# Gate and up chunks with ScalarE and VectorE in the program's order, and other pairs with seven products

## The chip, the cores and the metric

One core of a Trainium2 chip runs the kernel. The metric is device microseconds (us) of one execution, the median over runs; lower is better. TensorE is called PE here, VectorE DVE, ScalarE ACT, GpSimd POOL and SyncE SP, as in the profile.

## The reference

Two layers of a residual trunk on 256 tokens of width 2048, all in float32. Each layer normalises, projects, runs two kinds of attention, projects back, and then runs a SwiGLU. Only the SwiGLU matters here:

```python
def swiglu(h, w_gate, w_up, w_down):
    return (jax.nn.silu(h @ w_gate) * (h @ w_up)) @ w_down
...
        h = rms_norm(x, pre_ffn_norm[l])
        f = swiglu(h, w_gate[l], w_up[l], w_down[l])
        x = x + rms_norm(f, post_ffn_norm[l])
```

`w_gate` and `w_up` are 2048 x 5632, `w_down` is 5632 x 2048.

## The kernel before

**Precision.** Every float32 operand is split into a rounded part `hi` (written by ACT, L181 and L205) and a rest `lo = x - hi` (written by DVE, L182 and L207). A product of two blocks is three matmuls, hi by hi, hi by lo and lo by hi (`product`, L730). So each weight that PE uses goes through one ACT and one DVE instruction of 128x1024 first.

**Tiling of gate and up.** The 5632 columns are 11 chunks of 512. A chunk contracts 8 *K pairs* (`kp` 0 to 7) of 2 x 128 rows. For one pair the tokens (2 tiles of 128), the two row blocks and the two matrices make a 2 x 2 by 2 x 2 block product. `eight` (L837) takes it as 8 products, 24 matmuls. `seven` (L847) takes it as 7 products, 21 matmuls, from sums of blocks. The pairs in `SEVEN` (L36; chunk 0: `FIRST_SEVEN`, L37) go through `seven`. For them the sums of the tokens come once per layer from `pair_sums` (L830), placed in chunk 0 by `FORM_AT`, and the sums of the weights come from `mixed_weights` (L172) each time. The order of its steps on the two engines is:

1. ACT `hi` of gate (L205), DVE `lo` of gate (L207); ACT `hi` of the tile T (L181), DVE `lo` of T (L182). T is up with one half of gate added by a second DMA from POOL (`summed`, L164).
2. DVE L186 makes the sum t2 in T; DVE L187 and L188 overwrite the gate tile with two more sums.
3. ACT `Th` of t2 and DVE `Tl` of t2 (128x512); ACT `Th` and DVE `Tl` of the gate tile (128x1024). The first `Th` reads what L186 wrote, the second what L188 wrote, and each `Tl` reads its `Th`.

**Banks.** An odd and an even chunk use four PSUM banks each. The other four hold the shared products p1, p6, p7, q5 of the seven-product pairs. After the last such pair `shared_part` (L767) joins them with one ACT copy (L770) and four DVE instructions (L771 to L774); those banks then take the next chunk's sums.

**End of a chunk (L876 to L893).** Per token tile: DVE adds gate's bank (L880), ACT takes SiLU (L881), DVE adds up's bank (L882) and multiplies (L883). `flip`, started `DEFER_ACT` ticks later, transposes the result on PE (L889), into a bank that the next chunk's shared products use as well, and ACT copies it out (L890).

**Weights.** `fetch` (L149) puts the loads on SP's queue, 512 KB each, in the order of use; T loads are put up to `EARLY` places ahead. `feed` (L195) puts the splits ahead of the matmuls by `LOOKAHEAD` = 4 tiles, two pairs. Buffers: 4 `raw`, 6 `hi`, 6 `lo`, 3 T, 2 `Th`, 2 `Tl`. A buffer is given to a new tile when the old one's last reader is done.

**Down (L901 to L986).** Two halves of two column chunks each, 22 K pairs; the pairs in `DOWN_SEVEN` (L40) go through `seven_products`, the others through `down`. The last three pairs of the second half are the tail.

**What sets the order.** Tile's scheduler orders each engine's instructions by its own estimate of when they can start, unless a block is under `tc.manual_schedule`, in which the named engines keep the order in which the program records the instructions. Before, only the end of the output projection (L806) is under it.

Of the kernel before, what the change touches and what calls it, by code (L numbers as in the profile page):

```python
# [24 lines left out]
FF = 5632  # L25
CW = 512
# [6 lines left out]
URGENT = 50  # L33
TAIL = 3
KP_O = (4, 5, 6, 7, 0, 1, 2, 3)
SEVEN = (2, 4, 5, 6)  # L36
FIRST_SEVEN = (4, 6)  # L37
FIRST_ORDER = (0, 1, 3, 2, 4, 5, 6, 7)
FORM_AT = {1: 4, 3: 6, 4: 5, 5: 2}
DOWN_SEVEN = (2, 5, 8, 11, 14, 17)  # L40

WARM = 13
LEVEL = 232
# [7 lines left out]
def weight_order():  # L51
# [3 lines left out]
    def queue_pair(name, l, kp, c):  # L55
        order.append((name, l, kp, c))
        return len(order) - 1
# [3 lines left out]
    for l in range(L):  # L61
# [15 lines left out]
        for c in range(FF // CW):  # L77
            for kp in FIRST_ORDER if c == 0 else range(KT // 2):
                lay["gate"][c, kp] = queue_pair("w_gate", l, kp, c)
                lay["up"][c, kp] = queue_pair("w_up", l, kp, c)  # L80
                if kp in (FIRST_SEVEN if c == 0 else SEVEN):
                    sevens.add(lay["up"][c, kp])
        for half in range(2):
            for kp in range(FF // P // 2):
                for c in (2 * half, 2 * half + 1):
                    lay["down"][c, kp] = queue_pair("w_down", l, kp, c)
                if kp in DOWN_SEVEN:
                    sevens.add(lay["down"][2 * half + 1, kp])
# [17 lines left out]
def kernel(  # L106
# [30 lines left out]
    def four_banks(odd, names):  # L137
        makers = (bank, bank, bank, last_bank) if odd else (acc_bank,) * 4
        return [make(n) for make, n in zip(makers, names)]
# [75 lines left out]
    def weights(i, ahead):  # L215
        feed(i + 1 + ahead)
        return ready[i]
# [19 lines left out]
    def new_x_pool(nm):  # L237
        if x_pool[0] is not None:
            x_pool[0].release()
        x_pool[0] = tc.alloc_tile_pool(name=nm, bufs=1, side="right", reuse_waits="tile")  # L240
        return x_pool[0]
# [112 lines left out]
    def start(gen, n=1):  # L354
        running.append([clock[0] + n, gen])
# [381 lines left out]
    def token_sums(pool, spool, bufs, a11, a12, a21, a22, nm):  # L737

        s = pool.tile([P, 4, P], F32, tag="t2", name=f"s{nm}")
        nc.vector.tensor_tensor(out=s[:, 0, :], in0=a21, in1=a22, op=ALU.subtract)  # L740
        nc.vector.tensor_tensor(out=s[:, 1, :], in0=s[:, 0, :], in1=a11, op=ALU.subtract)
        nc.vector.tensor_tensor(out=s[:, 2, :], in0=a11, in1=a21, op=ALU.subtract)
        nc.vector.tensor_tensor(out=s[:, 3, :], in0=s[:, 1, :], in1=a12, op=ALU.add)
        sh = spool.tile([P, 4, P], F32R, tag="sh", bufs=bufs, name=f"sh{nm}")
        nc.scalar.activation(sh, s, AF.Copy)
        sl = spool.tile([P, 4, P], F32R, tag="sl", bufs=bufs, name=f"sl{nm}")
        nc.vector.tensor_tensor(out=sl, in0=s, in1=sh.bitcast(F32), op=ALU.subtract)
        return [(sh[:, j, :], sl[:, j, :]) for j in range(4)]
# [18 lines left out]
    def shared_part(extra, w):  # L767

        p1, p6, p7, q5 = extra
        nc.scalar.copy(w[0], p1)  # L770
        nc.vector.tensor_tensor(out=w[1], in0=p6, in1=w[0], op=ALU.add)  # L771
        nc.vector.tensor_tensor(out=w[2], in0=p7, in1=w[1], op=ALU.add)
        nc.vector.tensor_tensor(out=w[1], in0=q5, in1=w[1], op=ALU.subtract)
        nc.vector.tensor_tensor(out=w[3], in0=q5, in1=w[2], op=ALU.subtract)  # L774

    xT = None
    for l in range(L):
# [52 lines left out]
        def pair_sums(kp):  # L830
            f = pool.tile([P, 2, S], F32, tag="t2", name=f"f{l}_{kp}")
            for kk in range(2):
                st = xT[2 * kp + kk]
                nc.vector.tensor_tensor(out=f[:, kk, :], in0=st[:, 0, :].bitcast(F32), in1=st[:, 1, :].bitcast(F32), op=ALU.add)
            forms[kp] = token_sums(pool, gu, len(SEVEN), f[:, 0, 0:P], f[:, 1, 0:P], f[:, 0, P:S], f[:, 1, P:S], f"{l}_{kp}")

        def eight(banks, c, kp, toks, first, last):  # L837
            g, u = weights(plan[l]["gate"][c, kp], LOOKAHEAD), weights(plan[l]["up"][c, kp], LOOKAHEAD)
            for kk in range(2):
                st = xT[2 * kp + kk]  # L840
                for t in toks:
                    tick()
                    stat = (st[:, 0, t * P : (t + 1) * P], st[:, 1, t * P : (t + 1) * P])
                    for col, (hi, lo) in enumerate((g, u)):
                        product(banks[2 * t + col], stat, (hi[:, kk, :], lo[:, kk, :]), first and kk == 0, last and kk == 1)

        def seven(banks, extra, c, kp, first, last):  # L847
            hi, lo = weights(plan[l]["gate"][c, kp], LOOKAHEAD)
            m = weights(plan[l]["up"][c, kp], LOOKAHEAD)
            e, o = xT[2 * kp], xT[2 * kp + 1]  # L850
            a11, a12, a22 = (e[:, 0, 0:P], e[:, 1, 0:P]), (o[:, 0, 0:P], o[:, 1, 0:P]), (o[:, 0, P:S], o[:, 1, P:S])
            seven_products(banks, extra, forms[kp], a11, a12, a22, hi, lo, m, first, last)

        for c in range(FF // CW):
            banks = four_banks(c % 2, [f"c{q}_{l}_{c}" for q in ("11", "12", "21", "22")])
            mine = FIRST_SEVEN if c == 0 else SEVEN
            order = FIRST_ORDER if c == 0 else tuple(range(KT // 2))
            if c == 0:
                for t in range(NT):
                    for kp in order[:2]:  # L860
                        eight(banks, c, kp, (t,), kp == order[0], False)
                order = order[2:]
            extra = None
            for n, kp in enumerate(order):
                if c == 0 and n in FORM_AT:
                    pair_sums(FORM_AT[n])
                if kp not in mine:
                    eight(banks, c, kp, range(NT), kp == 0, kp == order[-1])
                    continue
                if kp == mine[0]:  # L870
                    extra = four_banks(1 - c % 2, [f"{q}_{l}_{c}" for q in ("p1", "p6", "p7", "q5")])
                seven(banks, extra, c, kp, kp == mine[0], kp == mine[-1])
                if kp == mine[-1]:
                    w = [pool.tile([P, CW], F32, tag="t2", name=f"w{j}_{l}_{c}") for j in range(4)]
                    shared_part(extra, w)
            at = pool.tile([P, 4, S], F32, tag="act", bufs=FF // CW, name=f"act{l}_{c}")  # L876
            act.append(at)
            sg = [w[0], w[2]]
            for t, u in ((0, w[1]), (1, w[3])):
                nc.vector.tensor_tensor(out=sg[t], in0=banks[2 * t], in1=sg[t], op=ALU.add)  # L880
                nc.scalar.activation(sg[t], sg[t], AF.Silu, scale=rs[t][:, 0:1])  # L881
                nc.vector.tensor_tensor(out=u, in0=banks[2 * t + 1], in1=u, op=ALU.add)  # L882
                nc.vector.scalar_tensor_tensor(out=sg[t], in0=u, scalar=rs[t][:, 0:1], in1=sg[t], op0=ALU.mult, op1=ALU.mult)  # L883

            def flip(sg=sg, at=at, c=c):
                for t in range(NT):
                    pb = (bank if c % 2 else acc_bank)(f"actT_ps{l}_{c}_{t}")
                    for j in range(4):
                        nc.tensor.transpose(pb[:, j * P : (j + 1) * P], sg[t][:, j * P : (j + 1) * P], ident)  # L889
                    nc.scalar.copy(at[:, :, t * P : (t + 1) * P], pb.rearrange("p (k q) -> p k q", k=4))  # L890
                    yield 1

            start(flip(), DEFER_ACT)  # L893
        gu.release()
        mix_pool[:] = new_x_pool(f"sums{l}"), 2, plan[l]["down"][3, FF // P // 2 - 1] + 1
        dn = tc.alloc_tile_pool(name=f"dn{l}", bufs=4, reuse_waits="tile")
# [6 lines left out]
        for half in range(2):  # L903
            split, forms = {}, {}

            def prep(kp):
# [7 lines left out]
                split[kp] = (jh, jl)  # L914
                if kp in DOWN_SEVEN:
                    a11, a12, a21, a22 = src[:, 0, 0:P], src[:, 1, 0:P], src[:, 0, P:S], src[:, 1, P:S]
# [23 lines left out]
            def down_seven(kp):  # L940
# [5 lines left out]
                m = weights(plan[l]["down"][cc[1], kp], LOOKAHEAD)  # L946
                seven_products(got, extra, forms[kp], a11, a12, a22, hi, lo, m, kp == DOWN_SEVEN[0], kp == DOWN_SEVEN[-1])

            tail = TAIL if half == 1 else 0
            for kp in range(nkp - tail):  # L950
                if kp not in DOWN_SEVEN:
                    down(kp, range(NT))
                    continue
                if kp == DOWN_SEVEN[0]:
                    extra = four_banks(half, [f"{q}_d{l}_{half}" for q in ("p1", "p6", "p7", "q5")])
                down_seven(kp)
                if kp == DOWN_SEVEN[-1]:
                    for t in range(NT):
# [84 lines left out]
```

## Time and profile before

| | |
|---|---|
| median of 3 runs | 2235.16 us (2232.64 to 2235.85) |
| the profiled execution | 2239.96 us, span 2237.9 us |
| granted clock of PE in it | 0.997 |
| PE busy | 2200.9 us, 98% of the span |
| DVE busy | 1789.1 us, 80% |
| ACT busy | 1309.5 us, 59% |
| DMA | 452 MB, mean 202 GB/s |
| gate and up, layer 0 and 1 | about 400 to 885 us and 1515 to 2005 us |
| down, layer 0 and 1 | about 885 to 1125 us and 2005 to 2238 us |

A matmul of 128x512 is listed with some 0.39 us, but the next one starts 0.227 us after it: matmuls overlap. A share of 98% for PE therefore hides little idle time, and its mean over all stages says nothing on how close DVE is to its limit in one of them. The stages have to be read one by one.

### The profile page before, as it was taken

What the parts mean: (1) busy time and instruction counts of PE and PEld (TensorE: products, weight loads), DVE (VectorE), ACT (ScalarE), POOL (GpSimd) and SP (SyncE); (2) the same over time, 40 slices, a digit from 0 to 9 for tenths busy, and PEclk for the clock granted to TensorE, in tenths of its full rate; (3) what the DMA queues carried; (4) which work ended last, traced back from release to release, by engine and by line L of the source; (5) the groups of instructions that cost most, each with busy time, mean ns of one, the idle gap of its engine ahead of it and who ended that gap; (6) DMA issues with size and microseconds to landing.
All of it is one profiled execution on the core that took longest, in us unless ns stands there. A gap on an engine that the chain in (4) does not pass through costs nothing.

```text
span 2237.9 us, 28440 instructions
## 1 busy us (share of the span) xinstructions
PE 2200.9 (98%) x10057; PEld 1802.2 (81%) x10057; DVE 1789.1 (80%) x2531; ACT 1309.5 (59%) x1937; POOL 132.0 (6%) x184
## 2 busy tenths in 40 slices
PE   9999999999999999999999999999999999999998
PEld 7888888777887888788878888887777887878886
DVE  6666555899988999989776665558999999998897
ACT  6545554665655656656565455546665566566664
POOL 1100000000000000000010000000000000000000
PEclk9999999999999999999999999999999999999999
DMA  8555455576776676766555544556677677666673
GB/s 290 189 167 164 160 190 183 186 223 209 226 242 199 212 251 190 228 214 205 193 184 171 168 162 160 188 186 192 206 218 237 218 222 234 221 203 222 203 232 132
DMA packets 133326, 452.05 MB, mean 202 GB/s; under 512 B 15296, under 2 KB 15808, under 8 KB 132672
## 3 DMA queue, kind: packets, MB, share of 16 engines
q1 hardware_dynamic: 117488, 421.91, 55.2%
q0 software_dynamic: 15552, 28.32, 7.6%
q8 instruction: 79, 1.29, 0.2%
q14 instruction: 63, 0.52, 0.1%
q10 hardware_dynamic: 144, 0.02, 0.0%
HBM read 448.09 MB, written 2.10 MB: 201 GB/s over the span
## 4 chain that ended last, share of the span: by engine, by line
PE 71%; DVE 13%; DMA 6%; issue 4%; ACT 4%; POOL 0%; DVEq 0%; ACTq 0%; SPq 0%; POOLq 0%
PE in L380 7%; PE in L382 7%; PE in L381 7%; DMA raw<-in_weights_in_turn_dram 5%; PE c L733 5%; PE c L734 5%; PE c L735 5%; PE dn L938 5%; PE dn L936 5%; PE dn L935 4%; DVE lo L207 3%; DVE Tl L182 2%; PE o L382 2%; PE o L381 2%; PE o L380 2%
## 5 line engine op out<-in xcount | busy, mean ns | idle before, releaser
L207 DVE TENSOR_TENSOR lo<-raw,hi 128x1024 fp32r<-128x1024 f32 x675 | 824.1, 1225 | 311.4 <-ACT hi L205 307.3
L205 ACT ACTIVATE hi<-raw 128x1024 fp32r<-128x1024 f32 x675 | 709.4, 1057 | 510.9 <-DMA raw<-in_weights_in_turn_dram 178.4
L733 PE MATMUL c<-hi,xF 128*128 128x512 f32 x820 | 321.0, 395 | 2.4 <-DVE w L774 1.3
L735 PE MATMUL c<-hi,xF 128*128 128x512 f32 x820 | 318.8, 391 | 0.0
L734 PE MATMUL c<-lo,xF 128*128 128x512 f32 x820 | 318.7, 389 | 0.0
L168 POOL DMA_DIRECT2D T<-in_weights_in_turn_dram x108 | 94.1, 871 | 1754.1 <-DMA T<-in_weights_in_turn_dram 821.8
L733 PEld LDWEIGHTS c<-hi,xF 128*128 128x128 f32 x820 | 154.0, 188 | 35.3 <-DVE w L774 2.5
L936 PE MATMUL dn<-lo,jh 128*128 128x512 f32 x464 | 180.8, 390 | 0.0
L935 PE MATMUL dn<-hi,jh 128*128 128x512 f32 x464 | 180.7, 389 | 0.0
L735 PEld LDWEIGHTS c<-hi,xF 128*128 128x128 f32 x820 | 153.9, 188 | 32.3
L734 PEld LDWEIGHTS c<-lo,xF 128*128 128x128 f32 x820 | 154.1, 188 | 30.9
L380 PE MATMUL in<-hi,xI 128*128 128x512 f32 x384 | 154.0, 401 | 0.2 <-ACT xI L321 0.2
L380 PE MATMUL in<-hi,xT 128*128 128x512 f32 x384 | 153.4, 400 | 0.2 <-ACT xT L616 0.2
L382 PE MATMUL in<-hi,xI 128*128 128x512 f32 x384 | 150.2, 391 | 0.3 <-DVE xI L326 0.3
L381 PE MATMUL in<-lo,xI 128*128 128x512 f32 x384 | 149.9, 390 | 0.5 <-DVE lo L207 0.5
L381 PE MATMUL in<-lo,xT 128*128 128x512 f32 x384 | 149.8, 390 | 0.5 <-DVE lo L207 0.5
L382 PE MATMUL in<-hi,xT 128*128 128x512 f32 x384 | 150.2, 391 | 0.0
L938 PE MATMUL dn<-hi,jl 128*128 128x512 f32 x464 | 143.3, 390 | 0.0
L182 DVE TENSOR_TENSOR Tl<-raw,Th 128x1024 fp32r<-128x1024 f32 x108 | 131.5, 1217 | 8.7 <-ACT Th L181 8.7
L181 ACT ACTIVATE Th<-raw 128x1024 fp32r<-128x1024 f32 x108 | 113.8, 1053 | 37.9 <-DVE raw L188 37.8
L182 DVE TENSOR_TENSOR lo<-T,hi 128x1024 fp32r<-128x1024 f32 x108 | 131.4, 1216 | 4.4 <-ACT hi L181 4.4
L181 ACT ACTIVATE Th<-T 128x512 fp32r<-128x512 f32 x108 | 67.9, 629 | 112.1 <-DVE T L186 96.3
(298 smaller groups left out, 4077.9 us busy)
## 6 DMA issues: line engine op xcount, KB each, us to landing
raw<-in_weights_in_turn_dram SPq DMA_DIRECT2D x675, 512.0 KB, 4.3
T<-in_weights_in_turn_dram SPq DMA_DIRECT2D x108, 512.0 KB, 4.4
T<-in_weights_in_turn_dram POOLq DMA_DIRECT2D x108, 256.0 KB, 6.5
xr<-in_x_columns_dram SPq DMA_DIRECT2D x8, 256.0 KB, 6.1
x<-in_x_dram SPq DMA_DIRECT2D x4, 512.0 KB, 9.2
gpost_mix<-in_post_mix_norm_dram SPq DMA_DIRECT2D x2, 1024.0 KB, 6.0
gpost_ffn<-in_post_ffn_norm_dram SPq DMA_DIRECT2D x2, 1024.0 KB, 8.1
out_dram<-x SPq DMA_DIRECT2D x8, 256.0 KB, 2.8
```

Of the source, the lines that this page charges most:

```text
L182: nc.vector.tensor_tensor(out=l, in0=w, in1=h.bitcast(F32), op=ALU.subtract)
L205: nc.scalar.activation(hi, raw, AF.Copy)
L207: nc.vector.tensor_tensor(out=lo, in0=raw, in1=hi.bitcast(F32), op=ALU.subtract)
L380: nc.tensor.matmul(a, sh, hi[:, kk, :], start=first and kk == 0, stop=False)
L381: nc.tensor.matmul(a, sh, lo[:, kk, :], start=False, stop=False)
L382: nc.tensor.matmul(a, sl, hi[:, kk, :], start=False, stop=last and kk == 1)
L733: nc.tensor.matmul(a, sh, hi, start=first, stop=False)
L734: nc.tensor.matmul(a, sh, lo, start=False, stop=False)
L735: nc.tensor.matmul(a, sl, hi, start=False, stop=last)
L935: nc.tensor.matmul(accs[c, t], sh, hi[:, kk, :], start=first, stop=False)
L936: nc.tensor.matmul(accs[c, t], sh, lo[:, kk, :], start=False, stop=False)
L938: nc.tensor.matmul(accs[c, t], sl, hi[:, kk, :], start=False, stop=last)
```

## The change

```diff
-SEVEN = (2, 4, 5, 6)
-FIRST_SEVEN = (4, 6)
+SEVEN = (2, 3, 5, 6)
+FIRST_SEVEN = (5, 6)
 FIRST_ORDER = (0, 1, 3, 2, 4, 5, 6, 7)
-FORM_AT = {1: 4, 3: 6, 4: 5, 5: 2}
-DOWN_SEVEN = (2, 5, 8, 11, 14, 17)
+FORM_AT = {1: 5, 2: 6, 4: 2, 5: 3}
+DOWN_SEVEN = (3, 6, 9, 12, 15, 18)
...
-        for c in range(FF // CW):
+        def chunk(c):
             banks = four_banks(c % 2, [f"c{q}_{l}_{c}" for q in ("11", "12", "21", "22")])
...
                 nc.vector.tensor_tensor(out=sg[t], in0=banks[2 * t], in1=sg[t], op=ALU.add)
                 nc.scalar.activation(sg[t], sg[t], AF.Silu, scale=rs[t][:, 0:1])
                 nc.vector.tensor_tensor(out=u, in0=banks[2 * t + 1], in1=u, op=ALU.add)
+            for t, u in ((0, w[1]), (1, w[3])):
                 nc.vector.scalar_tensor_tensor(out=sg[t], in0=u, scalar=rs[t][:, 0:1], in1=sg[t], op0=ALU.mult, op1=ALU.mult)
...
+        for c in range(FF // CW):
+            if c == 0:
+                chunk(c)
+                continue
+            with tc.manual_schedule(engines={mybir.EngineType.Activation, mybir.EngineType.DVE}):
+                chunk(c)
```

Chunks 1 to 10 of gate and up are recorded under `manual_schedule`, so in them ACT and DVE keep the program's order; PE, SP and POOL are still scheduled. The two multiplications at a chunk's end come after all four additions. In chunks 1 to 10 the pairs 2, 3, 5 and 6 take seven products in place of 2, 4, 5 and 6, in chunk 0 the pairs 5 and 6 in place of 4 and 6, and in down each such pair is one later. The number of pairs of each kind is unchanged, and so is the number of instructions of each engine. Lines from L880 on stand one line lower at the multiplication (L884) and the copy (L891), and seven lines lower from the down projection on.

## The prediction

> **What bounds the kernel now.** I read the page first, then the stages in windows, then who waited for whom, then the order in time of one chunk. The page gives one line per engine:
>
> ```profile
> PE 2200.9 (98%) x10057; PEld 1802.2 (81%) x10057; DVE 1789.1 (80%) x2531; ACT 1309.5 (59%) x1937; POOL 132.0 (6%) x184
> ```
>
> PE sets the end, and over the whole span VectorE has a fifth to spare. In the stage that the change touches this is not so. The windows below run from the end of chunk 0 to the end of chunk 10, layer 0 and layer 1 (columns: window, length, then busy time and count for PE, its weight loads, DVE, ACT, POOL, then granted clock, DMA share, GB/s). Below them is L880's wait, which stands once at each chunk's end, 11 times per layer, first and last start in us:
>
> ```profile
> 456.00:880.40 424.40, 417.52 (x1859) 341.32 (x1858) 393.89 (x469) 255.12 (x296) 32.17 (x37) 1.00 0.70 219
> 1570.00:1992.00 422.00, 416.32 (x1861) 340.51 (x1860) 393.78 (x470) 255.28 (x296) 32.17 (x37) 1.00 0.70 220
> ...
> L880 DVEq EVENT_SEMAPHORE  x11: 21/21/21, 455.7 to 880.2; - x11
> ...
> L880 DVEq EVENT_SEMAPHORE  x11: 21/21/21, 1570.1 to 1991.7; - x11
> ```
>
> Ten chunks take 424.5 and 421.6 us, so one takes 42.45 and 42.16 us. PE is idle for 0.69 and 0.57 of that. DVE is busy for 39.4 of it, 93%: it can lose 3 us per chunk and no more. What it loses now is nearly all one thing, and what PE waits for is what DVE and ACT deliver late (waits in the two windows, then in the two down stages: total us, times, longest):
>
> ```profile
> L207 DVE TENSOR_TENSOR lo<-raw,hi 128x1024 fp32r<-128x1024 f32 x120 | 146.0, 1218 | 27.5 <-ACT hi L205 27.4
> ...
> PE p L733 <- ACT Th L181: 2.8, 3, 1.5
> PE p L734 <- DVE Tl L182: 2.4, 4, 0.9
> ...
> PE p L734 <- DVE Tl L182: 2.7, 5, 0.9
> ...
> PE p_d L733 <- ACT Th L181: 2.3, 1, 2.3
> ...
> PE p_d L733 <- ACT Th L181: 2.5, 1, 2.5
> ```
>
> So gate and up run with PE and DVE nearly level, and a wait added on DVE shows in the time once it eats the 3 us.
>
> **The change part by part.** No engine gets more instructions. What moves is the order, and in the changed program as built DVE and ACT stand strictly in the recorded order through chunks 1 to 10. An engine takes its instructions in that order even when a later one could run:
>
> ```profile
> 659.33 0.56 ACT L770 COPY w<-p 128x512 f32<-128x512 f32 x1
> ...
> 659.53 1.21 DVE L207 TENSOR_TENSOR lo<-raw,hi 128x1024 fp32r<-128x1024 f32 x1
> 663.04 1.23 DVE L207 TENSOR_TENSOR lo<-raw,hi 128x1024 fp32r<-128x1024 f32 x1 [2.30 <-ACT hi L205]
> 664.18 0.68 DVE L771 TENSOR_TENSOR w<-p,w 128x512 f32<-128x512 f32 x1
> 664.90 0.69 DVE L772 TENSOR_TENSOR w<-p,w 128x512 f32<-128x512 f32 x1
> ...
> 660.69 0.40 PE L735 MATMUL p<-Th,sl 128*128 128x512 f32 x1
> ```
>
> L771 had its inputs by 661.1 (the copy's end and PE's last p product) and still stood behind `lo` until 664.18. So every wait in the new order is paid in full by whatever stands behind it. I work out one chunk of DVE, counting from start to start.
>
> *First, one pair with seven products.* In the new order its seven DVE instructions follow one another with nothing between them. The intervals:
>
> ```profile
> 674.25 1.22 DVE L182 TENSOR_TENSOR lo<-T,hi 128x1024 fp32r<-128x1024 f32 x1
> 675.51 0.69 DVE L186 TENSOR_TENSOR T<-T 128x512 f32<-128x512 f32 x1
> 676.24 0.69 DVE L187 TENSOR_TENSOR raw<-T,raw 128x512 f32<-128x512 f32 x1
> 676.85 0.68 DVE L188 TENSOR_TENSOR raw<-T,raw 128x512 f32<-128x512 f32 x1
> ...
> 643.16 0.68 DVE L188 TENSOR_TENSOR raw<-T,raw 128x512 f32<-128x512 f32 x1
> 643.77 0.69 DVE L182 TENSOR_TENSOR Tl<-T,Th 128x512 fp32r<-128x512 f32 x1
> 644.37 1.22 DVE L182 TENSOR_TENSOR lo<-T,hi 128x1024 fp32r<-128x1024 f32 x1
> 645.50 1.22 DVE L182 TENSOR_TENSOR Tl<-raw,Th 128x1024 fp32r<-128x1024 f32 x1
> ...
> 643.88 1.06 ACT L181 ACTIVATE Th<-raw 128x1024 fp32r<-128x1024 f32 x1 [0.49 <-DVE raw L188]
> ```
>
> A 128x1024 instruction takes 1.14, a 128x512 one 0.60; L186 comes 1.26 after the `lo` whose input it overwrites, and L187 0.73 after L186. The second `Th` can't start before L188 ends (0.68 + 0.04) and takes 1.06, so the second `Tl` starts 0.68 + 0.04 + 1.06 + 0.04 = 1.82 after L188. Before, another pair's `lo` filled that time (644.37). In the new order only the first `Tl` stands there, and DVE is free again after 1.20: it waits 0.62. The pair takes 1.14 + 1.26 + 0.73 + 0.60 + 1.82 + 1.14 = 6.69, and four take 26.8.
>
> *The rest of a chunk.* Eight `lo` of the other pairs at 1.14 are 9.1; the shared part is 0.72 + 3 x 0.60 = 2.5; the end, with its multiplications moved behind the four additions, is 4 x 0.60 + 2 x 0.66 = 3.7:
>
> ```profile
> 670.00 0.68 DVE L882 TENSOR_TENSOR w<-c,w 128x512 f32<-128x512 f32 x1
> 670.60 0.68 DVE L880 TENSOR_TENSOR w<-c,w 128x512 f32<-128x512 f32 x1
> 671.20 0.74 DVE L883 SCALAR_TENSOR_TENSOR w<-w,rs_ffn,w 128x512 f32<-128x512 f32 x1
> 671.86 0.68 DVE L882 TENSOR_TENSOR w<-c,w 128x512 f32<-128x512 f32 x1
> ```
>
> Moving the multiplications costs nothing: ACT's SiLU runs under the second token tile's additions; without that cover it would be one SiLU, some 0.7. Together 42.1, of which 2.5 are the four waits; without them 39.6, which agrees with the 39.4 busy of the window.
>
> *The copies of the flip.* In ACT's new order both stand behind the second `Th` of pair 3 and ahead of pair 4's `hi`:
>
> ```profile
> 677.72 1.05 ACT L181 ACTIVATE Th<-raw 128x1024 fp32r<-128x1024 f32 x1
> 678.67 1.05 ACT L890 COPY act<-actT_ps 128x512 f32<-128x512 f32 x2
> 679.61 1.07 ACT L205 ACTIVATE hi<-raw 128x1024 fp32r<-128x1024 f32 x1
> ```
>
> From L188 of pair 3: `Th` at 0.72, copies at +0.95, `hi` at +0.94 more, its end at 3.67, `lo` at 3.71. DVE is free at 1.82 + 1.14 = 2.96 and waits 0.75. The bank that the copies free late is also the next chunk's p7 and p6; PE's new order has put those products behind most of pair 3, so PE waits there about as long as for `Th` anyway, with DVE the later of the two.
>
> *A load that now comes late.* With 4 raw buffers given out in program order, up's tile of the next chunk's pair 0 gets the buffer of pair 6's gate, which is free only after pair 6's second `Tl`. Before, with `lo` of pair 7 ahead of that `Tl`, it got pair 7's. SP's queue holds nothing in front that is later (the T load before it waits for pair 6's first `Tl`). The landing times:
>
> ```profile
> raw<-in_weights_in_turn_dram SPq DMA_DIRECT2D x120, 512.0 KB, 5.0
> ...
> raw<-in_weights_in_turn_dram SPq DMA_DIRECT2D x675, 512.0 KB, 4.3
> ...
> DMA to landing us min/median/max: 4.4/6.8/7.6
> ```
>
> The first is the median of the layer 0 window, the second of the whole run, the third (of 6 loads issued around a chunk's end, 655 to 668 us) shows the worst. I take 5.0, because it is of this stage; ends 4.3 and 6.8. From the start of `Tl`: 1.21 + 5.0 + 0.05 + `hi` 1.06 + 0.04 = 7.36. In between stand only `Tl` itself and three `lo`, 4 x 1.14 = 4.56, so DVE waits 2.8 (2.1 to 4.6). The shared part and pair 1 stand behind it and wait too.
>
> The Trainium skill, page "DMA: Bandwidth & Descriptors", section "Anatomy of one DMA — SWDGE (gpsimd) path", fits 2.0 us plus bytes over 436 GB/s for another path. For 512 KB that is an estimate of 3.2 us, below every landing in the rows above; by it the wait would be 1.0, a chunk 43.9 and the time 2256.
>
> *The chunk.* 42.1 + 0.75 + 2.8 = 45.7 on DVE alone, against 42.45 and 42.16: 3.2 and 3.5 more. Ten chunks in each layer: 67.
>
> *What PE does meanwhile.* It waits for nothing that would delay DVE. By these rows a matmul takes 40 / 178 = 0.225:
>
> ```profile
> 880.00:920.00 40.00, 37.65 (x163) 30.76 (x162) 34.92 (x57) 24.51 (x31) 3.48 (x4) 0.96 0.72 219
> ...
> 960.00:1000.00 40.00, 40.00 (x178) 33.15 (x177) 30.02 (x34) 22.26 (x27) 1.22 (x2) 1.00 0.70 228
> ...
> 2000.00:2040.00 40.00, 37.48 (x165) 30.69 (x165) 37.01 (x57) 26.34 (x33) 3.33 (x5) 1.00 0.69 207
> ```
>
> After pair 6's last `Tl` (1.21 after its start) PE has some 11 matmuls of pair 6 and 24 of pair 7 to do, 7.9, and ends the chunk 9.1 after that start. DVE reaches the end's additions after 4.56 + 2.8 + 1.14 + 2.5 + 2.3 = 13.3. So PE ends a chunk 4.2 before DVE gets to it, where the two were level before. That lead is gained once in each layer and taken into down, for whose first two pairs the weights are split by then: 2 x 4.2 = 8.4 off.
>
> *Down.* Its first seven-product pair is pair 3 in place of 2, so its T, whose buffers come free with gate and up, has 24 x 0.225 = 5.4 more time than the 2.3 and 2.5 that PE waited for it. In the slices above PE did 15 and 13 matmuls fewer than 178, up to 3 us each, the wait and the slower clock after it. I take 5 for both. The later triples only shift; in the second half pair 18 now stands right before the tail, with the shared part's 2.5 of DVE under 18 tail matmuls (4.0), so I put that at nothing; uncovered it is 2.5 in each layer. Chunk 0's other pairs and sums I put at 0, between -1.5 and +1.5.
>
> *Sum.* 67 - 8.4 - 5 = +54. The profiled execution took 2239.96 with a span of 2237.9, 4.8 above the median 2235.16; I put the difference on the median: 2289.
>
> **The rivals.**
>
> *PE stays the bound, and the change is a gain.* If the waits of DVE fit into its 3 us per chunk, PE loses its idle time: 6.9 and 5.7 in the windows and 5 in down, 2218. For it: DVE now waits for `hi` 2.7 per chunk, and that could just change place. Against it: the chain L188, `Th`, `Tl` can't be shortened, and 39.6 + 2.5 + 0.75 alone is over 42.45. It decides from a DVE chunk under 41.8, PE's own (42.45 - 0.69).
>
> *The load is in time.* Only 42.87 per chunk: 4 + 7 more, less 2.8 of lead, less 5: 2239. Against it: the wait exists unless a load lands in 2.2, and none does.
>
> *Both late waits are smaller.* If the load lands in the run's median 4.3 and the copies find ACT free, the chunk is 42.1 + 2.1 = 44.2: 17.5 + 20.5 more, less 7 of lead, less 5: 2261. For it: the queue is emptier once DVE is slower. Against it: the stage's own median is 5.0, and ACT's order of copies and `hi` is fixed.
>
> *The load meets others.* Two more loads start within 2.3 us after it and a T load 1.8 before it. At 6.8 the chunk is 47.5: 50 + 53 - 12 - 5 = +86, 2321. For it: the row with 6.8; against: in that group three loads were issued ahead of the late one.
>
> **How the numbers follow.** My forecast has 0.74, the rivals in their order 0.05, 0.03, 0.08 and 0.10. The bounds of the landing time move the forecast by -13 and +32, the copies by -15 if ACT gets past them sooner, chunk 0 and the tail by up to 5. The range 2258 to 2318 takes these in, so the third rival too, and ends just short of the last. A measurement tells 0.2%, 4.5 us, from no change: faster 0.05 (the first rival), same 0.03 (the second), slower 0.92.
>
> **What would show it.** Right: L880's 11 waits lie 45 to 47 us apart; DVE waits for the second `Tl`'s `Th` about 0.6 x 80 times; each chunk has one wait of 2 us or more at the second of the two `lo` before L771, put down to a raw load by ACT; PE waits far more than 8 us per layer for `Th` and `Tl`; the p_d waits are gone. Wrong: L880 keeps 42 us, or those waits are there but shorter than the idle time they replace; or the lead of PE is lost in a wait at down's start.

## The result and the profile after

The changed kernel takes 2295.49 us (median of 4 runs, 2291.85 to 2297.81) against 2235.51 for the kernel before (4 runs): a ratio of 1.0269, 95% interval 1.0251 to 1.0287. It is 60 us slower. The profiled execution took 2295.16 us, on its median, with a span of 2293.2.

The page's engine line after the change, then its chain of waits (the work that ended last, followed back to what released it; shares of the span) after the change and, in the last line, before:

```profile
PE 2228.4 (97%) x10057; PEld 1807.7 (79%) x10057; DVE 1804.1 (79%) x2531; ACT 1308.7 (57%) x1937; POOL 132.2 (6%) x184
...
PE 55%; DVE 22%; ACT 8%; issue 7%; DMA 7%; POOL 0%; DVEq 0%; ACTq 0%; SPq 0%; POOLq 0%
...
PE 71%; DVE 13%; DMA 6%; issue 4%; ACT 4%; POOL 0%; DVEq 0%; ACTq 0%; SPq 0%; POOLq 0%
```

In the shares of busy time nothing seems to have happened: PE is at 97%, DVE at 79%, as before. But DVE, ACT and the DMAs now carry 37% of the chain that ended last, where they carried 23%. The stage shows it. Windows of the changed kernel from the end of chunk 0 to the end of chunk 10, layer 0 and 1 (columns as before):

```profile
455.00:908.60 453.60, 433.23 (x1876) 345.90 (x1875) 400.86 (x470) 252.98 (x294) 32.23 (x37) 0.98 0.69 204
1595.80:2051.60 455.80, 434.45 (x1877) 345.78 (x1876) 400.77 (x470) 254.47 (x295) 32.19 (x37) 0.99 0.69 203
```

and L880's wait, one at each chunk's end, in the same kernel:

```profile
L880 DVEq EVENT_SEMAPHORE  x11: 21/21/21, 454.9 to 908.5; - x11
...
L880 DVEq EVENT_SEMAPHORE  x11: 21/21/21, 1595.7 to 2051.5; - x11
```

A chunk takes 45.36 and 45.58 us, where it took 42.45 and 42.16. DVE runs the same instructions (470 and 469 recorded in layer 0's window; 40.1 us busy a chunk, 39.4 before), and PE is now idle for 2.0 a chunk instead of 0.69. What DVE and PE wait for in the two windows (total us, times, longest):

```profile
DVE lo L207 <- ACT hi L205: 27.7, 19, 3.2
DVE Tl L182 <- ACT Th L181: 21.0, 40, 0.5
PE c L733 <- ACT Th L181: 17.5, 11, 1.9
...
DVE lo L207 <- ACT hi L205: 30.0, 19, 4.3
DVE Tl L182 <- ACT Th L181: 21.0, 40, 0.5
PE c L733 <- ACT Th L181: 16.8, 10, 1.9
```

`lo` waits about as long as before (27.4 in layer 0). The 21.0 of `Tl` are new (1.3 before), 40 times in each layer, four in each chunk. The order of one chunk on DVE in the changed kernel (start, duration, in brackets the idle time before it and its releaser):

```profile
686.32 1.22 DVE L207 TENSOR_TENSOR lo<-raw,hi 128x1024 fp32r<-128x1024 f32 x1
...
690.04 0.68 DVE L188 TENSOR_TENSOR raw<-T,raw 128x512 f32<-128x512 f32 x1
690.64 0.69 DVE L182 TENSOR_TENSOR Tl<-T,Th 128x512 fp32r<-128x512 f32 x1
691.85 1.22 DVE L182 TENSOR_TENSOR Tl<-raw,Th 128x1024 fp32r<-128x1024 f32 x1 [0.53 <-ACT Th L181]
692.99 1.22 DVE L207 TENSOR_TENSOR lo<-raw,hi 128x1024 fp32r<-128x1024 f32 x1
...
698.52 1.23 DVE L182 TENSOR_TENSOR Tl<-raw,Th 128x1024 fp32r<-128x1024 f32 x1 [0.52 <-ACT Th L181]
700.45 3.50 DVE L207 TENSOR_TENSOR lo<-raw,hi 128x1024 fp32r<-128x1024 f32 x3 [0.70 <-ACT hi L205]
...
714.94 1.23 DVE L182 TENSOR_TENSOR Tl<-raw,Th 128x1024 fp32r<-128x1024 f32 x1 [0.53 <-ACT Th L181]
716.08 3.49 DVE L207 TENSOR_TENSOR lo<-raw,hi 128x1024 fp32r<-128x1024 f32 x3
721.64 1.23 DVE L207 TENSOR_TENSOR lo<-raw,hi 128x1024 fp32r<-128x1024 f32 x1 [2.07 <-ACT hi L205]
722.78 0.68 DVE L771 TENSOR_TENSOR w<-p,w 128x512 f32<-128x512 f32 x1
...
731.49 1.22 DVE L207 TENSOR_TENSOR lo<-raw,hi 128x1024 fp32r<-128x1024 f32 x1
```

From the first `lo` of one chunk to that of the next are 45.17 us. All three kinds of wait can be read off: 0.53 ahead of each long `Tl`, 0.70 behind pair 3, 2.07 ahead of the shared part. On ACT the two larger ones are these, the copies of the flip and a raw load:

```profile
698.40 1.06 ACT L891 COPY act<-actT_ps 128x512 f32<-128x512 f32 x2
699.34 2.96 ACT L205 ACTIVATE hi<-raw 128x1024 fp32r<-128x1024 f32 x3
...
720.55 1.06 ACT L205 ACTIVATE hi<-raw 128x1024 fp32r<-128x1024 f32 x1 [2.80 <-DMA raw<-in_weights_in_turn_dram]
```

SP's queue issued that load at 716.19, when pair 6's `Tl` (714.94 to 716.17) had freed the buffer:

```profile
716.19 7.03 SPq L159 DMA_DIRECT2D raw<-in_weights_in_turn_dram  x5
```

### The profile page after: what moved, and what is told of

Same layout as the page of the kernel before. It is cut to its first block, busy times and chain, and to the rows that moved or that the text cites. A ratio compares the mean times of both kernels' runs of the same rounds, so it can differ in the third digit from the quotient of the medians.

```text
span 2293.2 us, 28456 instructions
## 1 busy us (share of the span) xinstructions
PE 2228.4 (97%) x10057; PEld 1807.7 (79%) x10057; DVE 1804.1 (79%) x2531; ACT 1308.7 (57%) x1937; POOL 132.2 (6%) x184
## 4 chain that ended last, share of the span: by engine, by line
PE 55%; DVE 22%; ACT 8%; issue 7%; DMA 7%; POOL 0%; DVEq 0%; ACTq 0%; SPq 0%; POOLq 0%
PE in L380 7%; PE in L382 7%; PE in L381 7%; DVE lo L207 6%; DMA raw<-in_weights_in_turn_dram 5%; PE dn L943 4%; PE dn L942 4%; PE dn L945 4%; DVE lo L182 4%; ACT Th L181 3%; PE o L382 2%; PE o L381 2%; PE o L380 2%; ACT hi L205 2%; DVE T L186 2%
## 5 line engine op out<-in xcount | busy, mean ns | idle before, releaser
L207 DVE TENSOR_TENSOR lo<-raw,hi 128x1024 fp32r<-128x1024 f32 x675 | 815.4, 1225 | 309.7 <-ACT hi L205 305.8
L205 ACT ACTIVATE hi<-raw 128x1024 fp32r<-128x1024 f32 x675 | 701.2, 1057 | 445.3 <-DMA raw<-in_weights_in_turn_dram 178.4
L182 DVE TENSOR_TENSOR Tl<-raw,Th 128x1024 fp32r<-128x1024 f32 x108 | 132.2, 1224 | 47.3 <-ACT Th L181 47.3
```

The lines of the kernel that those rows point to most:

```text
L182: nc.vector.tensor_tensor(out=l, in0=w, in1=h.bitcast(F32), op=ALU.subtract)
L205: nc.scalar.activation(hi, raw, AF.Copy)
L207: nc.vector.tensor_tensor(out=lo, in0=raw, in1=hi.bitcast(F32), op=ALU.subtract)
```

## The experiments

"Chunk" is the distance of L880's waits in layer 0 and layer 1, taken as above. It comes from one profiled execution of each kernel; in bare_wait and fill_both that one took 6 us less than the median. Ratios are to the kernel before on the same chip, where it took 2233.9 to 2237.4 us.

| kernel | median us | ratio (95% interval) | chunk us |
|---|---|---|---|
| changed | 2295.49 | 1.0269 (1.0251 to 1.0287) | 45.36, 45.58 |
| order_only | 2294.07 | 1.0258 (1.0243 to 1.0274) | 45.21, 45.25 |
| pairs_only | 2261.67 | 1.0110 (1.0093 to 1.0127) | 43.90, 43.99 |
| act_only | 2289.01 | 1.0236 (1.0220 to 1.0251) | 45.73, 45.59 |
| dve_only | 2358.54 | 1.0546 (1.0524 to 1.0567) | 48.78, 48.78 |
| bare_wait | 2327.51 | 1.0418 (1.0401 to 1.0435) | 47.04, 46.90 |
| fill_tl | 2350.24 | 1.0517 (1.0501 to 1.0534) | 48.54, 48.66 |
| shared_first | 2276.47 | 1.0182 (1.0167 to 1.0197) | 44.61, 44.61 |
| copies_early | 2277.83 | 1.0189 (1.0173 to 1.0204) | 45.12, 44.61 |
| down_only | 2231.50 | 0.9990 (0.9979 to 1.0000) | 42.12, 42.05 |
| fill_both | 2257.31 | 1.0104 (1.0087 to 1.0121) | 43.20, 43.68 |
| shared_copies | 2256.58 | 1.0095 (1.0080 to 1.0110) | 43.65, 43.54 |
| three_fixed | 2222.44 | 0.9944 (0.9932 to 0.9956) | 41.79, 41.73 |

### Which part of the change: order_only, pairs_only

order_only is the changed kernel with the old pairs, in gate, up and down:

```diff
-SEVEN = (2, 3, 5, 6)
-FIRST_SEVEN = (5, 6)
+SEVEN = (2, 4, 5, 6)
+FIRST_SEVEN = (4, 6)
...
-FORM_AT = {1: 5, 2: 6, 4: 2, 5: 3}
-DOWN_SEVEN = (3, 6, 9, 12, 15, 18)
+FORM_AT = {1: 4, 3: 6, 4: 5, 5: 2}
+DOWN_SEVEN = (2, 5, 8, 11, 14, 17)
```

> The order of ACT and DVE alone, with the pairs of before everywhere. Theory (DVE's three waits per chunk, 0.53 us at each second Tl, 0.7 us behind the copies, 2.1 to 2.3 us for up's tile of pair 0): the waits at Tl and for the load stay, the copies stand one pair later in ACT's order and cost 0.4 instead of 0.7, so a chunk is near 45.0 us and the time 2280 to 2295 us. Rival (the other pairs cost the time, since two of them now follow each other at 2 and 3): 2230 to 2245 us.

pairs_only is the changed kernel without the fixed order:

```diff
-            with tc.manual_schedule(engines={mybir.EngineType.Activation, mybir.EngineType.DVE}):
-                chunk(c)
+            chunk(c)
```

> The other pairs and the multiplications moved, without the fixed order. Theory: DVE's gaps are filled by the scheduler again, 2225 to 2240 us, chunks near 42.3 us. Rival (the pairs cost it): 2275 us or more.

order_only came as expected. The fixed order alone costs 57 us, nearly as much as the whole change, and has the same waits in its layer 0 window:

```profile
DVE lo L207 <- ACT hi L205: 26.2, 19, 3.2
DVE Tl L182 <- ACT Th L181: 21.0, 40, 0.5
```

It also rules out PE's waits and its clock as the cause. After the change PE waits 17.5 for `Th` in that window and its granted clock is 0.98; in order_only it waits 0.3 and the clock is 1.00, and a chunk takes the same 45.2.

pairs_only missed: without the fixed order the new pairs still cost 24 us. There the `Tl` waits are gone, but `lo` waits 39.0 in the layer 0 window (27.4 before), since ACT waits longer for raw loads (47.3 before):

```profile
ACT hi L205 <- DMA raw<-in_weights_in_turn_dram: 77.0, 42, 4.0
```

So under the scheduler the kernel loses by late loads, and under the fixed order the pairs make no difference (2294 and 2295). What brings the loads late there, the pairs or the moved multiplications, was not separated, nor why the fixed order hides this loss.

### Which engine's order: act_only, dve_only

```diff
-            with tc.manual_schedule(engines={mybir.EngineType.Activation, mybir.EngineType.DVE}):
+            with tc.manual_schedule(engines={mybir.EngineType.Activation}):
```

> Only ACT keeps the program's order, DVE is scheduled. Theory: the waits at Tl and the late load come from DVE's order, so most of the loss is gone: 2235 to 2262 us. Rival (the loss comes from ACT's order, its copies and its Th that PE waits for 17 us in each layer): 2280 us or more.

dve_only names `mybir.EngineType.DVE` alone in the same place.

> Only DVE keeps the program's order, ACT is scheduled. Theory: Tl stands behind Tl with nothing between and the raw buffer of pair 6 is still free late, so at most the copies' 0.7 us per chunk, 14 us, is gained: 2276 to 2297 us. Rival (ACT's order): 2235 to 2255 us.

Both missed. With ACT alone in the program's order the time is nearly that of the change. In act_only's trace DVE's splits stand in the recorded order all the same, though the scheduler placed them; only two `lo` per chunk stand elsewhere, inside the shared part and not behind it. So the wait of the long `Tl` for `Th` is there 40 times again in its layer 0 window, 21.0 in all. The rival's time came true; of its two reasons, order_only rules out PE's wait for `Th`.

With DVE alone fixed it is worst. ACT then stands in an order of the scheduler's, and in the layer 0 window `Tl` waits for it 53 times, 47.7 in all and up to 2.5.

So neither order alone is harmless: ACT's brings nearly the whole loss with it, and DVE's without ACT's is worse than both.

### The price of the wait for Th: bare_wait

The long `Th` and `Tl` are put ahead of the short ones, so that nothing stands between L188 and the long `Tl`:

```diff
+        split(th[:, 0:2, :], tl[:, 0:2, :], g)
         split(th[:, 2, :], tl[:, 2, :], t2)
-        split(th[:, 0:2, :], tl[:, 0:2, :], g)
```

> The changed kernel, with the long Th and Tl of the gate tile ahead of the short ones of t2, everywhere. Theory: the chain from L188 by Th to Tl now has nothing beside it on DVE, so each of the pairs 2, 3 and 5 waits 0.6 us longer; at pair 6 the same 0.6 us comes off the wait for the load. 20 x 1.8 = 36 us more: 2322 to 2340 us. Rival (PE sets the pace and these waits of DVE are hidden): within 8 us of the changed kernel.

It came as expected. In its layer 0 window `Tl` waits 46.7, 25.7 more than after the change, and `lo` 19.2, 8.5 less, because the late load has more time:

```profile
DVE Tl L182 <- ACT Th L181: 46.7, 40, 1.2
...
DVE lo L207 <- ACT hi L205: 19.2, 19, 3.4
```

That is 17.2 more in layer 0, where ten chunks took 16.8 more (470.4 against 453.6). Here a wait on DVE is paid in full.

### Filling the wait, first try: fill_tl

For pairs 2, 3 and 5 the long `Tl` goes behind the next pair's first `lo` on DVE. ACT's order stays. `hold` is set in chunks 1 to 10, `final` holds the tiles of pair 6, and `put_late` writes the deferred `Tl`.

```diff
-        split(th[:, 0:2, :], tl[:, 0:2, :], g)
+        if hold[0] and i not in final:
+            nc.scalar.activation(th[:, 0:2, :], g, AF.Copy)
+            late.append((tl[:, 0:2, :], g, th[:, 0:2, :]))
+        else:
+            split(th[:, 0:2, :], tl[:, 0:2, :], g)
...
             nc.vector.tensor_tensor(out=lo, in0=raw, in1=hi.bitcast(F32), op=ALU.subtract)
+            put_late()
```

> The changed kernel, with the second Tl of pairs 2, 3 and 5 put behind the next pair's first lo on DVE. Theory: three of the four waits of 0.53 us in a chunk are gone, 20 x 1.6 = 32 us: 2258 to 2272 us. Rival (PE sets the pace: it waits 17 us per layer for Th, which is not moved, and gets these Tl 0.6 us later): 2290 us or more.

The miss was large: 55 us slower than the change instead of some 30 faster. The reason stands in DVE's and ACT's rows of this kernel:

```profile
707.93 0.68 DVE L191 TENSOR_TENSOR Tl<-T,Th 128x512 fp32r<-128x512 f32 x1
710.09 1.23 DVE L220 TENSOR_TENSOR lo<-raw,hi 128x1024 fp32r<-128x1024 f32 x1 [1.47 <-ACT hi L218]
```

```profile
708.04 1.06 ACT L200 ACTIVATE Th<-raw 128x1024 fp32r<-128x1024 f32 x1 [0.69 <-DVE raw L197]
709.01 1.04 ACT L218 ACTIVATE hi<-raw 128x1024 fp32r<-128x1024 f32 x1
```

The filler `lo` needs the next `hi`, and on ACT that `hi` stands behind the long `Th`. So DVE waits for both ACT instructions, 1.47, instead of 0.53 for the first; behind pair 3, where the copies stand in between too, 2.44. With 1.48 behind pair 5 that is 5.4 a chunk, where the change paid 3 x 0.53 and 0.70 in the same places; the difference is 3.1, and a chunk grew by 3.2. The filler was free of the wait on DVE but not on ACT.

### The two later waits: shared_first, copies_early

shared_first records the chunk's shared part ahead of the late `lo`, by looking one tile less far at the last pair with seven products:

```diff
-            m = weights(plan[l]["up"][c, kp], LOOKAHEAD)
+            m = weights(plan[l]["up"][c, kp], LOOKAHEAD - (c > 0 and last))
```

> The changed kernel, with the shared part put ahead of up's tile of the next chunk's pair 0. Theory: the 2.1 to 2.3 us wait for that load is covered by the shared part's 2.5 us, 20 x 2.2 = 44 us less, of which some 4 go to the lead that PE then does not take into down: 2250 to 2262 us. Rival (PE sets the pace): 2285 us or more; rival (the load lands as late as before and the wait only moves to the next lo): 2285 us or more too, but with a DVE wait of about 2 us at another lo.

copies_early starts the flip at once and puts its copies ahead of pair 3's first `Th`:

```diff
         split(hi, lo, u)
+        while out_copies:
+            at, t, pb = out_copies.pop(0)
+            nc.scalar.copy(at[:, :, t * P : (t + 1) * P], pb.rearrange("p (k q) -> p k q", k=4))
...
-            start(flip(), DEFER_ACT)
+            start(flip(), 1 if c < FF // CW - 1 else DEFER_ACT)
```

> The changed kernel, with the flip's transposes recorded four ticks earlier and its two copies put ahead of pair 3's first Th on ACT. Theory: ACT has 2.4 us idle there, so the 0.70 us wait of DVE at pair 4 is gone and nothing takes its place: 14 us less, 2277 to 2286 us. Rival (the bank that the copies free is what holds PE and PE the rest): 2265 us or less. Rival (the copies cost nothing now): 2292 us or more.

copies_early came as expected: in its layer 0 window `lo` waits 9 times and no longer 19, and PE's wait for `Th` in the c products falls from 17.5 to 0.8:

```profile
DVE lo L212 <- ACT hi L210: 26.2, 9, 3.6
DVE Tl L184 <- ACT Th L183: 21.0, 40, 0.5
...
PE c L738 <- ACT Th L183: 0.8, 1, 0.8
```

But each of the 9 waits for the late load is now 2.9. shared_first gained 19 of the 33 to 45 that were expected, and so fell between the theory and both rivals. `lo` still waits 15.4 in 24 places; 6.9 of that are the copies, ten times 0.69, and 8.5 in 14 places are loads, where the change had 20.8 in 9. And PE now waits for the end of the chunk on DVE before it transposes (layer 0 window of shared_first):

```profile
DVE lo L207 <- ACT hi L205: 15.4, 24, 1.7
...
PE actT_ps L890 <- DVE w L884: 7.3, 8, 1.7
```

### Together, and the filler with ACT's order: shared_copies, fill_both

shared_copies is both edits above.

> The changed kernel with two edits that were each tried alone (2276 and 2278): the chunk's shared part ahead of the late lo, and act's copies recorded earlier, ahead of pair 3's first Th. Theory: they take away different waits, the late raw load and the copies, so their gains add up: 2295 - 19 - 18 = 2258 (2252 to 2265), chunks of 43.8. Rival: transposes recorded earlier wait longer for the silu product that shared_first made late for PE (7.3 us in a layer), and the gains don't add: 2268 to 2285, with PE waiting over 12 us in a layer for w.

fill_both defers the long `Th` too, behind the next `hi` (`late_hi` writes it, `late_lo` the `Tl`):

```diff
-        split(th[:, 0:2, :], tl[:, 0:2, :], g)
+        if hold[0] and i not in final:
+            late.append((th[:, 0:2, :], tl[:, 0:2, :], g))
+        else:
+            split(th[:, 0:2, :], tl[:, 0:2, :], g)
...
             nc.scalar.activation(hi, raw, AF.Copy)
+            late_hi()
...
             nc.vector.tensor_tensor(out=lo, in0=raw, in1=hi.bitcast(F32), op=ALU.subtract)
+            late_lo()
```

> The changed kernel, chunks 1 to 10; for pairs 2, 3 and 5 the long Th is put behind the next pair's first hi on ACT, and the long Tl behind the next pair's first lo on DVE. Theory: the wait of 0.5 before the long Tl is one of place, DVE reaches it before ACT has ended Th; with lo in between, and its hi already made, three of the four go in each chunk, 20 x 3 x 0.53 = 32 us: 2260 to 2272, with Tl waiting some 10 times and not 40 in a layer. Rival, the order tried with DVE's filler alone (2350) shows that any such move only shifts the wait to lo: 2285 or more, with lo waiting for hi over 30 us in a layer.

Both theories held, with a little more gained in fill_both than expected. The gains of the two edits in shared_copies add up (39 of 37). In fill_both's layer 0 window only pair 6's `Tl` waits, 10 times; what is left is the late load and the copies:

```profile
DVE lo L224 <- ACT hi L221: 23.8, 19, 2.9
DVE Tl L195 <- ACT Th L194: 5.3, 10, 0.5
```

From fill_tl to fill_both the long `Th` changes its place on ACT, and that is worth 93 us.

### Down's pairs alone: down_only

```diff
-DOWN_SEVEN = (2, 5, 8, 11, 14, 17)
+DOWN_SEVEN = (3, 6, 9, 12, 15, 18)
```

> The kernel before with down's other pairs (3, 6, ... 18) alone; gate and up as before. The prediction gave down 5 us less, since PE's waits for Th and Tl there (5.1 and 5.2 us in the two layers) would go. Theory now: the changed kernel still waits for down's first Th (2.8 and 1.3 us), because the T load issued where down begins shares the queues with the raws and takes as long; so 2233 to 2237, within 2 us of the kernel before. Rival, the prediction's own term: 2229 to 2232.

The time, 2231.5, lies in the rival's range. But the kernel before took 2233.88 beside it, so the gain is 2.4, between the two expectations, and its interval runs from 0 to 4.7: a small gain, and not the 5 of the prediction. The trace puts 1.3 of it in down: from layer 0's last wait of L880 (877.5) to layer 1's first (1566.9) are 689.4 us (689.9 before), from layer 1's last (1987.4) to the end of the span (2232.8) 245.4 (246.2).

### All three: three_fixed

The changed kernel with shared_first, copies_early and fill_both.

> The changed kernel with all three edits: shared part ahead of the late lo, copies early, the long Th and Tl of pairs 2, 3 and 5 behind the next hi and lo. Theory: they take away three different waits, 18.5 + 18 + 38 of the 60 us; adding up they give 2221, but with 40.1 us of work a chunk DVE is then no later than PE, whose 42.1 to 42.4 a chunk come back as the bound: 2222 to 2236, as fast as the kernel before, chunks of 42.0 to 42.7, DVE waiting under 15 us in a layer. Rival: the waits take each other's place again, as the filler on DVE alone showed: 2245 to 2256, with lo waiting for hi over 20 us in a layer.

It came as expected, at the lower end: 2222.44 us, 0.9944 of the kernel before (0.9932 to 0.9956), the fastest of all. Its window over the ten chunks of layer 0:

```profile
455.40:873.30 417.90, 414.94 (x1856) 339.94 (x1855) 397.37 (x467) 249.09 (x293) 32.18 (x37) 1.00 0.70 221
```

and its waits in that window:

```profile
DVE w L794 <- PE p L758: 6.8, 6, 1.1
...
DVE Tl L197 <- ACT Th L196: 5.3, 10, 0.5
DVE lo L229 <- ACT hi L226: 3.8, 5, 1.4
```

PE is idle for 0.30 a chunk, and DVE's longest item is now a wait for PE: PE is the bound again. So the fixed order isn't slower by itself. The order that the program recorded had three kinds of wait in it, and an order without them is at least as fast as the scheduler's.

## Why the prediction was right, and where not

It gave 2289 with a range of 2258 to 2318, from waits that make DVE the bound of a chunk; 2295.5 was measured, and the mechanism is the forecast one. Some of its terms were off, and the errors partly cancel:

- **The pair of seven: right.** From 686.32 to 692.99 are 6.67 (6.69 forecast). The long `Tl` starts 1.81 after L188 (1.82). The profile calls 0.53 of it idle, since it counts from the end of an instruction of 0.68; from start to start, where 0.60 are usual, 0.61 are lost. fill_both takes three of the four waits away, bare_wait makes them more than twice as long, and the time follows.
- **The rest of a chunk: right.** The shared part takes 2.72 (from 722.78 to the `lo` at 725.50; 2.5 forecast), the end 3.72 (from L880 at 727.77 to the `lo` at 731.49; 3.7).
- **The copies: right.** `lo` starts at 700.45 in place of 698.52 + 1.14 = 699.66: 0.79 (0.75).
- **The late load: the right place, a little too dear.** Pair 6's `Tl` released it, as forecast, but ACT could start 4.36 after the issue, where 5.0 were taken for the landing. DVE waited 721.64 - 716.08 - 3 x 1.14 = 2.14 in this chunk, not 2.8; there are nine such waits in a layer, not ten, since down follows the last chunk; the 18 are 1.6 to 4.3 long and 2.4 in the mean, 44 in all. shared_first shows the size only in part, since the wait spread to other `lo`. The estimate of 3.2 for 512 KB, from the fit that the Trainium skill, page "DMA: Bandwidth & Descriptors", section "Anatomy of one DMA — SWDGE (gpsimd) path", gives for another path, lies below the 4.36; the measurement decides.
- **The chunk: right.** 45.36 and 45.58 (45.7): 29.1 + 34.2 = 63.3 more in the two layers, where 67 were forecast. Errors cancel in it: the load cost 12 less than 20 x 2.8, the shared part and the copies together some 5 more, and the other 3 were not traced.
- **PE's lead: nearly right.** The first matmul of down on PE's timeline after the change:

```profile
905.82 0.39 PE L942 MATMUL dn<-hi,jh 128*128 128x512 f32 x1
```

  That is 2.7 ahead of L880 at 908.5; before, PE went over 1.1 behind it (881.3 and 880.2). 3.8 in each layer (layer 1 gives the same) are 7.6 in both (8.4 forecast). The two ends of the difference were each over a microsecond off: PE ahead by 2.7 and not 4.2 after the change, behind by 1.1 and not level before.
- **Down: the step that failed.** The prediction took 5 off, because T for the first pair with seven products would have 5.4 us more and PE's wait for it would go. The stretch from layer 0's last wait of L880 to layer 1's first gained 2.7, and that from layer 1's last to the end 4.5 (687.2 and 241.7 us after, 689.9 and 246.2 before). That is 7.2 in all, less than the lead alone: without the lead the two stretches, with down in both, cost 0.4. PE's wait is still there, 2.8 and 1.3 in the two layers after the change:

```profile
PE p_d L733 <- ACT Th L181: 2.8, 1, 2.8
...
PE p_d L733 <- ACT Th L181: 1.3, 1, 1.3
```

T's way shows where the 5.4 went. First the rows of T at the start of down in layer 0 after the change (durations in ns, first and last start):

```profile
L167 SPq DMA_DIRECT2D T<-in_weights_in_turn_dram x2: 328/376/425, 906.0 to 911.2; - x2
L168 POOL DMA_DIRECT2D T<-in_weights_in_turn_dram x2: 862/868/875, 912.1 to 920.1; - x2
L181 ACT ACTIVATE hi<-T x1: 1061/1061/1061, 921.1 to 921.1; 128x1024 fp32r<-128x1024 f32 x1
...
L181 ACT ACTIVATE Th<-T x1: 630/630/630, 926.0 to 926.0; 128x512 fp32r<-128x512 f32 x1
```

and the same before:

```profile
L167 SPq DMA_DIRECT2D T<-in_weights_in_turn_dram x3: 328/328/426, 881.5 to 898.5; - x3
L168 POOL DMA_DIRECT2D T<-in_weights_in_turn_dram x2: 865/868/872, 887.2 to 888.2; - x2
L181 ACT ACTIVATE hi<-T x1: 1061/1061/1061, 891.5 to 891.5; 128x1024 fp32r<-128x1024 f32 x1
...
L181 ACT ACTIVATE Th<-T x1: 633/633/633, 895.6 to 895.6; 128x512 fp32r<-128x512 f32 x1
```

In both, T's load starts as PE enters down. From there to its `hi` it took 10.0 before and 15.1 after: until POOL issued the accumulation 5.7 and 6.1, from there to `hi` 4.3 and 9.0. From `hi` to `Th` it took 4.1 before and 4.9 after. That accounts for the wait: 2.3 + 5.1 + 0.8 - 5.4 = 2.8. In layer 1 the same two ways grew by 3.3 (10.1 to 13.4) and 0.8: 2.5 + 3.3 + 0.8 - 5.4 = 1.2, where 1.3 were measured. So the extra pair of time was there, but T's way became as much longer, most of it by the accumulating transfer.

Why that transfer became slower is argued, not shown. After the change SP's queue put four raw loads behind T's within 5 us; before, the next one came 13 us later. In down_only two raw loads were issued around the transfer, and it took 8.8 and 6.5 us to `hi` in the two layers (4.3 and 3.7 before). And in the changed kernel's trace the accumulating transfers that were issued with one load of SP's queue still in flight landed after a median of 4.5 us (42 of 108), those issued with two or more after 7.2 (62); the four with none, at 5.6, don't fit in. The rest agrees, but no run took the loads away.

In down_only, with the chunks as before, the wait shrinks to 1.0 for `Th` and 1.2 for `Tl` in layer 0 and 1.2 in layer 1, and the gain is 1.3 in the trace and 2.4 by the medians: the term was too large even there, and in the changed kernel nothing was left of it.

- **The base.** Span against span the change costs 55.3 (63.3 - 7.2, and 0.8 less up to the end of layer 0's chunk 0), and the sum said 53.6. That they lie so close is partly luck: the chunks cost 3.7 less than forecast, and 8.0 came off elsewhere where 13.4 had been taken off. The other 4.8 of the 6.5 between 2289 and 2295.5 come from the profiled execution of before, which lay that far above its median. In down_only, whose ACT, DVE and PE instructions keep the same order as before up to layer 0's last chunk, the ten chunks took 421.2 us and not 424.5. That suggests that most of the 4.8 lay in this very stage, and that a chunk of layer 0 grew by some 3.2 against a usual execution, not 2.9.
- **The rivals.** "PE stays the bound" fell with a chunk of 45.4, far above the 41.8 from which it starts, and "the load is in time" with the wait of 2.07 for that load. "Both late waits smaller" had the load nearly right (2.1) and the copies wrong (0.79, not 0). "The load meets others" does not hold for the mean chunk, which stays far below 47.5; one of the 18 waits, 4.3, comes near its 4.6.

## What to carry to other kernels

When two engines hand tiles to and fro and both keep the program's order, record independent work between the steps on both of them: a filler on one engine is of no use while the instruction that it needs stands behind the wait on the other (2350 against 2257 us). Before fixing an order, add up each chain from start to start and ask for each instruction whose buffer it frees, and for which load; on an engine with 7% to spare small waits add up (three of the four 0.5 us in a chunk were worth 38 of the 60 us here). A wait that is expected to vanish because its reader comes later is not gone until its transfer has been timed under the new traffic.

## What the runs showed of the hardware

The accumulating transfer of 256 KB from POOL took 4.3 us from its issue to the reader's start at layer 0's down before, and 9.0 after the change, where loads of 512 KB were in flight on SP's queue; in the changed kernel's trace such transfers landed after a median of 4.5 us with one of those loads in flight at the issue (42) and 7.2 with two or more (62). And ten chunks with the same instructions in the same order on ACT, DVE and PE took 424.5 us in one profiled execution (before, layer 0) and 421.2 in another (down_only): a sum made against one execution carries such a difference with it.
